# Both column blocks of the HGRN value input made in one opening pass of a float32 decoder block

## The chip, the cores and the metric

One core of one Trainium2 chip runs the whole kernel in one launch. The metric is device time in microseconds (us), lower is better. The kernel before was timed in three runs. One further execution was recorded by the hardware profiler, and all rows shown below come from it.

## The reference

The reference is a decoder block in float32 on 256 tokens of width 1024. Cut to what matters here:

```python
h = rmsnorm(x, attn_norm_g)
proj = h @ w_in                                   # 1024 -> 9216 columns
hq, hf, hi, hg, aq, ak, av, gl = split(proj)      # eight blocks of 1024, the last of 2048
y_hg = hgrn2_mix(hq, hf, hi, hg, lb, out_gain) @ w_branch_hg    # linear recurrence
att  = moba_attention(rmsnorm(aq), rmsnorm(ak), av, rel_table)  # causal, 8 heads of 128
y_at = att @ w_branch_attn
gates = sigmoid(gl)
x = x + (gates[0] * y_hg + gates[1] * y_at) @ w_out
h2 = rmsnorm(x, ffn_norm_g)
x = x + (silu(h2 @ w_gate) * (h2 @ w_up)) @ w_down              # width 2816
```

`hi` is the value input of the recurrence (columns 2048 to 3071 of `w_in`), `hg` its output gate, `av` the attention values, `gl` the two branch gates. The division by the row norm is taken out of the products: they run on `x` times the channel gain, and each result is scaled afterwards by a factor per token, `rx`.

## The kernel before

**Arithmetic.** Each float32 operand is split into a rounded part (`hi`) and the rest (`lo`), and three products (hi hi, hi lo, lo hi) stand for one. For every piece of weight that arrives (`wraw`), ScalarE (ACT) makes the rounded part `whi` by a copy, VectorE (DVE) makes the rest `wlo` by a subtraction, and TensorE (PE) multiplies. `XT` holds the two parts of the input, eight tiles of 128 channels (`kt` 0 to 7).

**Blocks.** `tok_block` (L76) makes 256 tokens by 512 columns with 48 matmuls into two banks of the accumulator. `feat_block` (L86) makes 512 columns by 256 tokens in 32 pairs of matmuls into four banks. `load_w` (L58) fetches a block in two halves of 1 MiB, through three buffers each of `wraw`, `whi` and `wlo`. The accumulator has four banks named `pw` for these blocks, and two each of `ph` and `pa` for smaller work.

**Opening (L119 to L161).** While the input arrives, the first column block of `hi` (columns 2048 to 2559, banks `V0`) is made tile by tile: for each `kt` SyncE (SP) fetches 256 KiB of weight and 128 KiB of `x`. Then `F0`, the first half of the `hf` block, is begun (L209). The rows of `x` (`xtok`, L212) come behind the weights of `F0`; ACT squares and sums them (L216), `rinv` (L180) takes the root, and `rx` follows. `spread` (L185) brings `rx` over to the other axis by two small matmuls on `dg`. `put_tok` (L225) moves `V0` out of its banks into `V`.

**Middle (L498 to L547).** The recurrence is worked off in levels (`hgrn_level`, L315), each a short chain over ACT, PE and DVE, and one `tok_block` stands between two levels so that PE has work. The second column block of `hi` is one of these fillers (L512), then come the two blocks of `Va`, two of the output gate `sg`, and the branch gates `G`. `hgrn_out` (L372) makes the output `o`, sums its squares and takes `ro`; `hgrn_gate` (L394) multiplies `o` by `ro` and `sg` on DVE and transposes it on PE.

**Order.** Every engine works its own queue in a fixed order. The order is fixed when the program is built, by a scheduler that starts from the order of the code. DMAs issued by SP carry one of eight counters in turn, so a DMA waits until the one eight places ahead of it has landed.

Of the kernel before, what the change touches and what calls it, by code (L numbers as in the profile page):

```python
# [7 lines left out]
F32 = mybir.dt.float32  # L8
# [6 lines left out]
P = 128  # L15
# [12 lines left out]
def tile_hgrn2_moba_block(ctx: ExitStack, tc: tile.TileContext, xm, xT, vecs, table, onehot,  # L28
# [22 lines left out]
    def part(pair, k, m):  # L51
        return pair[k // 4][:, k % 4, m, :]
# [23 lines left out]
    def tok_block(w, c0, act, parts=(4, 4), bank=pw):  # L76
        ps = [bank(), bank()]
        for kt, wh, wl in chunks(w, c0, 512, parts):
            for tb in range(2):
                ts = slice(tb * P, (tb + 1) * P)  # L80
                nc.tensor.matmul(ps[tb], part(act, kt, 0)[:, ts], wh, start=(kt == 0), stop=False)  # L81
                nc.tensor.matmul(ps[tb], part(act, kt, 0)[:, ts], wl, start=False, stop=False)  # L82
                nc.tensor.matmul(ps[tb], part(act, kt, 1)[:, ts], wh, start=False, stop=(kt == KT - 1))  # L83
        return ps
# [31 lines left out]
    vec = const.tile([P, 35], F32, name="vec")  # L116
    xTr = big.tile([P, KT, S], F32, name="xTr", tag="T1")
    XT = [big.tile([P, 4, 2, S], F32R, name=f"XT{i}", tag=("XH", "XL")[i]) for i in range(2)]
    raws = [wp.tile([P, 4, 512], F32, name="wraw") for _ in range(2)]  # L119
    nc.scalar.dma_start(vec, vecs)  # L120
    nc.sync.dma_start(raws[0][:, 0, :], w_in[0:P, 2048:2560])
    nc.sync.dma_start(xTr[:, 0:1, :], xT[:, 0:1, :])
    ones = const.tile([P, P], F32, name="ones")
    nc.vector.memset(ones, 1.0)
    root = small.tile([P, 1], F32, name="root")
# [7 lines left out]
    x_parts = [(k, 1) for k in range(6)] + [(6, 2)]
    whs = [wp.tile([P, 4, 512], F32R, name="whi") for _ in range(2)]
    wls = [wp.tile([P, 4, 512], F32R, name="wlo") for _ in range(2)]
    for k0, n in x_parts:
        xs = slice(k0, k0 + n)
        ks = slice(k0 % 4, k0 % 4 + n)
        if k0 > 0:
            nc.sync.dma_start(raws[k0 // 4][:, ks, :],  # L140
                              w_in[k0 * P:(k0 + n) * P, 2048:2560].rearrange("(k p) c -> p k c", p=P))
            nc.sync.dma_start(xTr[:, xs, :], xT[:, xs, :])
    for k0, n in x_parts:
        raw, wh, wl = raws[k0 // 4], whs[k0 // 4], wls[k0 // 4]
        ks = slice(k0 % 4, k0 % 4 + n)
        nc.scalar.copy(wh[:, ks, :], raw[:, ks, :])
        for kt in range(k0, k0 + n):
            x_hi, x_lo = part(XT, kt, 0), part(XT, kt, 1)
            if kt == 0:
                nc.vector.tensor_scalar_mul(x_hi, xTr[:, kt, :], vec[:, kt:kt + 1])  # L150
            else:
                nc.scalar.mul(x_hi, xTr[:, kt, :], vec[:, kt:kt + 1])
            nc.vector.scalar_tensor_tensor(x_lo, xTr[:, kt, :], vec[:, kt:kt + 1], x_hi.bitcast(F32),
                                           op0=OP.mult, op1=OP.subtract)
        nc.vector.tensor_sub(wl[:, ks, :], raw[:, ks, :], wh[:, ks, :].bitcast(F32))
        for kt in range(k0, k0 + n):
            i = kt % 4
            for am, w in ((0, wh), (0, wl), (1, wh)):
                for tb in range(2):
                    nc.tensor.matmul(V0[tb], part(XT, kt, am)[:, tb * P:(tb + 1) * P], w[:, i, :],  # L160
                                     start=(kt == 0 and am == 0 and w is wh), stop=(kt == KT - 1 and am == 1))  # L161

    ones_r = const.tile([P, P], F32R, name="ones_r")
    nc.gpsimd.tensor_copy(ones_r, ones)
# [43 lines left out]

    F0 = feat_block(w_in, 1024, XT, cut=2)  # L209

    xtok = big.tile([P, 2, D], F32, name="xtok", tag="T2")
    nc.sync.dma_start(xtok, xm.rearrange("(b p) c -> p b c", p=P))  # L212
    ss = small.tile([P, 2], F32, name="ss")
    junk = big.tile([P, D], F32, name="junk", tag="T12")
    for tb in range(2):
# [9 lines left out]
    def put_tok(dst, ps, half):  # L225
        for tb in range(2):
            nc.scalar.mul(dst[:, tb, half * 512:(half + 1) * 512], ps[tb], rx[:, tb:tb + 1])

    put_tok(V, V0, 0)


    K = big.tile([P, 2, H, P], F32, name="K", tag="T2")
# [73 lines left out]
    def hgrn_diag_put(qkh, qkl):  # L306
        for tb in range(2):
            for g in range(2):
                bank = ph().rearrange("p (h t) -> p h t", h=4)
                for m, part in enumerate((qkh, qkl)):  # L310
                    nc.tensor.matmul(bank, ones_r, part[:, tb, 4 * g:4 * g + 4, :], start=(m == 0), stop=(m == 1))
                nc.vector.tensor_mul(A[:, tb, 4 * g:4 * g + 4, :], bank,
                                     ident.unsqueeze(1).to_broadcast([P, 4, P]))
# [374 lines left out]
```

## Time and profile before

| | us |
|---|---|
| median of three runs | 505.94 (504.81 to 505.97) |
| the profiled execution, its own time | 506.59 |
| its span in the profile | 504.5 |
| PE busy | 496.2 |
| DVE busy | 332.9 |
| ACT busy | 283.0 |

The span is the time between the first and the last instruction recorded; 2.1 us of the execution's own time lie around it. The profiled execution was 0.65 us slower than the median. PE is the engine of the multiplications; a PE row's duration covers the pipeline, so two matmuls in a row overlap and their cost is read from the distance of their starts.

### The profile page before, as it was taken

The page shows a single profiled execution, that of the slowest core. Times are in us where ns is not written, and L with a number is a line of the kernel's source. Part 1 is how long each engine was busy: PE and PEld are TensorE (multiplying, and loading weights), DVE is VectorE, ACT ScalarE, POOL GpSimd, SP SyncE. Part 2 cuts the span into 40 slices and gives each one's busy share as a digit, 9 for nine tenths or more (in the row PEclk, how much of TensorE's full clock was granted, in tenths as well). Part 3 has the DMA queues.
Part 4 walks back from the last instruction along what each step waited for, and adds up shares of the span by engine and source line. Part 5 has one row for each costly group of instructions (what it writes and reads, how often), then busy time and mean ns, then how long its engine had stood idle before and what let it go on. Part 6 is the DMA issues. An engine that isn't in the chain of part 4 may idle for free.

```text
span 504.5 us, 6639 instructions
## 1 busy us (share of the span) xinstructions
PE 496.2 (98%) x2674; PEld 417.0 (83%) x2674; DVE 332.9 (66%) x380; ACT 283.0 (56%) x418; POOL 20.4 (4%) x41
## 2 busy tenths in 40 slices
PE   8899999999999999999999999999999999999996
PEld 6688888788888888888888887888888888888885
DVE  6569998977698643564447567867645746566372
ACT  5597556787569547954443335675535535544350
POOL 9102200000000000000000000000000000000000
PEclk9999999999999999999999999999999999999999
DMA  7966957525424644185465554566555655653522
GB/s 239 380 219 191 350 177 243 168 83 177 159 75 148 202 161 129 39 307 194 166 211 206 166 168 169 171 199 203 176 172 191 213 176 173 210 161 96 193 88 83
DMA packets 44126, 91.20 MB, mean 181 GB/s; under 512 B 1944, under 2 KB 5048, under 8 KB 44096
## 3 DMA queue, kind: packets, MB, share of 16 engines
q1 hardware_dynamic: 43216, 88.12, 52.6%
q0 software_dynamic: 736, 2.65, 1.7%
q8 instruction: 21, 0.34, 0.3%
q14 instruction: 9, 0.07, 0.0%
q10 hardware_dynamic: 144, 0.02, 0.0%
HBM read 89.70 MB, written 1.07 MB: 180 GB/s over the span
## 4 chain that ended last, share of the span: by engine, by line
PE 93%; DMA 2%; ACT 2%; DVE 1%; SPq 0%; issue 0%; DVEq 0%
PE pw L99 21%; PE pw L81 13%; PE pw L82 13%; PE pw L83 13%; PE pw L98 9%; PE acc L610 4%; PE acc L608 4%; PE acc L609 4%; DMA wraw<-w_in 2%; PE ph L332 2%; PE pw L101 1%; PE ph L382 1%; PE pa L492 1%; PE pa L81 1%; PE pa L82 1%; PE pa L83 1%
## 5 line engine op out<-in xcount | busy, mean ns | idle before, releaser
L56 DVE TENSOR_TENSOR wlo<-wraw,whi 128x2048 fp32r<-128x2048 f32 (+1 forms) x83 | 182.1, 2196 | 111.5 <-ACT whi L55 111.1
L55 ACT CAST whi<-wraw 128x2048 fp32r<-128x2048 f32 (+1 forms) x83 | 151.7, 1829 | 117.9 <-PE pw L83 42.2
L99 PE MATMUL pw<-x2T,whi 128*128 128x512 f32 x352 | 121.9, 398 | 0.0
L98 PE MATMUL pw<-x2T,wlo 128*128 128x256 f32 x308 | 86.5, 281 | 0.0
L81 PE MATMUL pw<-whi,XT 128*128 128x512 f32 x192 | 75.8, 395 | 0.0
L82 PE MATMUL pw<-wlo,XT 128*128 128x512 f32 x192 | 75.2, 392 | 0.0
L83 PE MATMUL pw<-whi,XT 128*128 128x512 f32 x192 | 74.9, 390 | 0.0
L99 PEld LDWEIGHTS pw<-x2T,whi 128*128 128x128 f32 x352 | 63.5, 188 | 12.5
L98 PEld LDWEIGHTS pw<-x2T,wlo 128*128 128x128 f32 x308 | 58.2, 189 | 1.8
L99 PE MATMUL pw<-XT,whi 128*128 128x512 f32 x128 | 44.7, 399 | 0.2 <-DVE Fg L111 0.2
L81 PEld LDWEIGHTS pw<-whi,XT 128*128 128x128 f32 x192 | 36.1, 188 | 7.5
L83 PEld LDWEIGHTS pw<-whi,XT 128*128 128x128 f32 x192 | 36.1, 188 | 7.5
L82 PEld LDWEIGHTS pw<-wlo,XT 128*128 128x128 f32 x192 | 36.1, 188 | 7.3
L608 PE MATMUL acc<-whi,hT 128*128 128x512 f32 x88 | 34.3, 390 | 0.0
L610 PE MATMUL acc<-whi,hT 128*128 128x512 f32 x88 | 34.3, 390 | 0.0
L609 PE MATMUL acc<-wlo,hT 128*128 128x512 f32 x88 | 34.2, 389 | 0.0
L98 PE MATMUL pw<-XT,wlo 128*128 128x256 f32 x112 | 31.5, 281 | 0.0
L99 PEld LDWEIGHTS pw<-XT,whi 128*128 128x128 f32 x128 | 23.3, 188 | 5.1 <-DVE Fg L111 0.5
L98 PEld LDWEIGHTS pw<-XT,wlo 128*128 128x128 f32 x112 | 21.2, 189 | 0.8
L609 PEld LDWEIGHTS acc<-wlo,hT 128*128 128x128 f32 x88 | 16.5, 188 | 3.5
L610 PEld LDWEIGHTS acc<-whi,hT 128*128 128x128 f32 x88 | 16.5, 188 | 3.5
L608 PEld LDWEIGHTS acc<-whi,hT 128*128 128x128 f32 x88 | 16.5, 188 | 3.2
(226 smaller groups left out, 684.2 us busy)
## 6 DMA issues: line engine op xcount, KB each, us to landing
wraw<-w_in SPq DMA_DIRECT2D x32, 1024.0 KB, 5.2
wraw<-w_down SPq DMA_DIRECT2D x11, 1024.0 KB, 4.9
wraw<-w_gate SPq DMA_DIRECT2D x10, 1024.0 KB, 5.2
wraw<-w_up SPq DMA_DIRECT2D x10, 1024.0 KB, 5.1
wraw<-w_at SPq DMA_DIRECT2D x4, 1024.0 KB, 5.0
wraw<-w_hg SPq DMA_DIRECT2D x4, 1024.0 KB, 5.2
wraw<-w_out SPq DMA_DIRECT2D x4, 1024.0 KB, 5.1
wraw<-w_in SPq DMA_DIRECT2D x5, 512.0 KB, 9.2
```

The source lines that it names most:

```text
L55: nc.scalar.copy(hi, src)
L56: nc.vector.tensor_sub(lo, src, hi.bitcast(F32))
L81: nc.tensor.matmul(ps[tb], part(act, kt, 0)[:, ts], wh, start=(kt == 0), stop=False)
L82: nc.tensor.matmul(ps[tb], part(act, kt, 0)[:, ts], wl, start=False, stop=False)
L83: nc.tensor.matmul(ps[tb], part(act, kt, 1)[:, ts], wh, start=False, stop=(kt == KT - 1))
L98: nc.tensor.matmul(ps[ct][:, 0:S], lo[:, i, cs], part(act, kt, 0), start=False, stop=False)
L99: nc.tensor.matmul(ps[ct], hi[:, i, cs], both, start=(kt == 0), stop=(kt == KT - 1))
L101: nc.tensor.matmul(ps[ct][:, 0:S], lo[:, i, cs], part(act, kt, 0), start=False, stop=False)
L332: nc.tensor.matmul(o, KP[:, h, qs], t, start=True, stop=True)
L608: nc.tensor.matmul(acc[tb][half], act[:, j, 0, ts], hi[:, i, cs], start=st, stop=False)
L609: nc.tensor.matmul(acc[tb][half], act[:, j, 0, ts], lo[:, i, cs], start=False, stop=False)
L610: nc.tensor.matmul(acc[tb][half], act[:, j, 1, ts], hi[:, i, cs], start=False, stop=en)
```

## The change

The opening now makes all 1024 columns of `hi`, in four banks (`V0`, `V1`), in one loop over `kt`. Its buffers hold two `kt` of 1024 columns in place of four of 512, which is the same size. From `kt` 2 on, a tile of weight comes as one DMA of 512 KiB. `xtok` is fetched after the weights of `kt` 5 and before those of `kt` 6. `kt` 6 and 7 are multiplied for both halves after both are announced. The second `put_tok` of `V` follows the first. In the middle the filler at L512 is gone, and the blocks behind it move up by one: `Va` takes its place, the output gate takes that of `Va`, the first block of branch gate 1 that of the output gate's second. `Va`, `sg` and `G1` live in other buffers for it. `hgrn_diag_put` alternates between banks `ph` and `pa`.

```diff
+    def first(kind, name):
+        return wp.tile([P, 2, D], kind, name=name)
...
+    xtok = big.tile([P, 2, D], F32, name="xtok", tag="T2")
...
-    nc.sync.dma_start(raws[0][:, 0, :], w_in[0:P, 2048:2560])
+    nc.sync.dma_start(raws[0][:, 0, 0:512], w_in[0:P, 2048:2560])
     nc.sync.dma_start(xTr[:, 0:1, :], xT[:, 0:1, :])
+    nc.sync.dma_start(raws[0][:, 0, 512:D], w_in[0:P, 2560:3072])
...
+    V1 = [pw(), pw()]
+    whs, wls = [], []
+
+    def first_products(ps, half, kt):
+        i, hs = kt % 2, slice(half * 512, (half + 1) * 512)
+        wh, wl = whs[kt // 2], wls[kt // 2]
+        for am, w in ((0, wh), (0, wl), (1, wh)):
+            for tb in range(2):
+                nc.tensor.matmul(ps[tb], part(XT, kt, am)[:, tb * P:(tb + 1) * P], w[:, i, hs],
+                                 start=(kt == 0 and am == 0 and w is wh), stop=(kt == KT - 1 and am == 1))
+
+    for kt in range(KT):
+        i = kt % 2
+        if i == 0:
+            if kt > 0:
+                raws.append(first(F32, "wraw"))
+            whs.append(first(F32R, "whi"))
+            wls.append(first(F32R, "wlo"))
+        raw, wh, wl = raws[-1], whs[-1], wls[-1]
+        ks = slice(kt * P, (kt + 1) * P)
+        if kt > 0:
+            nc.sync.dma_start(xTr[:, kt:kt + 1, :], xT[:, kt:kt + 1, :])
+            for hs in ((slice(0, 512), slice(512, D)) if kt < 2 else (slice(0, D),)):
+                nc.sync.dma_start(raw[:, i, hs], w_in[ks, 2048 + hs.start:2048 + hs.stop])
+        if kt == 5:
+            nc.sync.dma_start(xtok, xm.rearrange("(b p) c -> p b c", p=P))
+        x_hi, x_lo = part(XT, kt, 0), part(XT, kt, 1)
+        if kt == 0:
+            nc.scalar.copy(wh[:, i, 0:512], raw[:, i, 0:512])
+            nc.vector.tensor_scalar_mul(x_hi, xTr[:, kt, :], vec[:, kt:kt + 1])
+        else:
+            nc.scalar.mul(x_hi, xTr[:, kt, :], vec[:, kt:kt + 1])
+            nc.scalar.copy(wh[:, i, 0:512], raw[:, i, 0:512])
+        nc.vector.scalar_tensor_tensor(x_lo, xTr[:, kt, :], vec[:, kt:kt + 1], x_hi.bitcast(F32),
+                                       op0=OP.mult, op1=OP.subtract)
+        nc.scalar.copy(wh[:, i, 512:D], raw[:, i, 512:D])
+        for hs in (slice(0, 512), slice(512, D)):
+            nc.vector.tensor_sub(wl[:, i, hs], raw[:, i, hs], wh[:, i, hs].bitcast(F32))
+        for half in range(2):
+            for k in ((), (6, 7))[kt // 7] if kt > 5 else (kt,):
+                first_products((V0, V1)[half], half, k)
...
-    xtok = big.tile([P, 2, D], F32, name="xtok", tag="T2")
-    nc.sync.dma_start(xtok, xm.rearrange("(b p) c -> p b c", p=P))
...
     put_tok(V, V0, 0)
+    put_tok(V, V1, 1)
...
-                bank = ph().rearrange("p (h t) -> p h t", h=4)
+                bank = (ph, pa)[g]().rearrange("p (h t) -> p h t", h=4)
...
-    put_tok(V, tok_block(w_in, 2048 + 512, XT), 1)
+    Va = big.tile([P, 2, D], F32, name="Va", tag="T1")
+    put_tok(Va, tok_block(w_in, 6144, XT), 0)
     S0, S1 = scores(qtok, qss, kT)
     hgrn_level(3)
-    Va = big.tile([P, 2, D], F32, name="Va", tag="T8")
-    put_tok(Va, tok_block(w_in, 6144, XT), 0)
+    put_tok(Va, tok_block(w_in, 6144 + 512, XT), 1)
     softmax("a", S0, P)
     softmax("b", S1, S)
     hgrn_level(4)
-    put_tok(Va, tok_block(w_in, 6144 + 512, XT), 1)
+    sg = big.tile([P, 2, D], F32, name="sg", tag="T8")
...
+    gate_block(0)
     PT0, PT1 = probs_T(S0, S1)
     hgrn_level(5)
-    sg = big.tile([P, 2, D], F32, name="sg", tag="T1")
-
-    def gate_block(half):
-        ps = tok_block(w_in, 3072 + half * 512, XT)
-        for tb in range(2):
-            nc.scalar.activation(sg[:, tb, half * 512:(half + 1) * 512], ps[tb], AF.Silu, scale=rx[:, tb:tb + 1])
-
-    gate_block(0)
+    gate_block(1)
     aT = values(Va, PT0, PT1)
     hgrn_level(6)
-    gate_block(1)
+
+
+    G[1] = big.tile([P, 2, D], F32, name="G1", tag="T11")
+    branch_gate(1, 0)
     A01 = hgrn_cross()
     o, ro = hgrn_out(A01)
-
-
-    G = [None, None]
-    for br in (1, 0):
-        G[br] = big.tile([P, 2, D], F32, name=f"G{br}", tag=("T5", "T6")[br])
-        for half in range(2):
-            ps = tok_block(w_in, 7168 + br * D + half * 512, XT)
-            for tb in range(2):
-                nc.scalar.activation(G[br][:, tb, half * 512:(half + 1) * 512], ps[tb], AF.Sigmoid,
-                                     scale=rx[:, tb:tb + 1])
-            if br == 1 and half == 0:
-                oT = hgrn_gate(o, ro, sg)
+    branch_gate(1, 1)
+    oT = hgrn_gate(o, ro, sg)
+    G[0] = big.tile([P, 2, D], F32, name="G0", tag="T6")
+    branch_gate(0, 0)
+    branch_gate(0, 1)
```

**PE, at the end of `hi`.** `pw` are the banks of `hi` (`XT_75` holds `kt` 4 to 7), then of `F0` (`XT_74` holds `kt` 0 to 3), and `ph<-dg` is the matmul of `spread`. Before:

```order
L160 MATMUL pw<-whi,XT_75 128x512 x4
L160 MATMUL pw<-wlo,XT_75 128x512 x2
L160 MATMUL pw<-whi,XT_75 128x512 x2
L99 MATMUL pw<-XT_74,whi 128x512
L101 MATMUL pw<-XT_74,wlo 128x256
L98 MATMUL pw<-XT_74,wlo 128x256
```

Now:

```order
L149 MATMUL pw<-whi,XT_75 128x512 x3
L149 MATMUL pw<-wlo,XT_75 128x512 x2
L149 MATMUL pw<-whi,XT_75 128x512 x2
L210 MATMUL ph<-dg,ones 128x128
L149 MATMUL pw<-whi,XT_75 128x512 x3
L149 MATMUL pw<-wlo,XT_75 128x512 x2
L149 MATMUL pw<-whi,XT_75 128x512 x3
L149 MATMUL pw<-wlo,XT_75 128x512 x2
L149 MATMUL pw<-whi,XT_75 128x512 x2
L210 MATMUL ph<-dg,ones 128x128
L99 MATMUL pw<-XT_74,whi 128x512
```

The first matmul of `spread` stands between the products of `kt` 6 and those of `kt` 7; before, both stood behind all of `F0`.

**ACT, around the squares of `xtok`.** Before:

```order
L152 ACTIVATE XT_75<-xTr,vec 128x256 x2
L55 CAST whi<-wraw 128x1024 x4
L110 COPY Fg<-pw 128x2x128
L216 ACTIVATE junk,ss<-xtok 128x1024
L182 ACT_TABLE_LOAD
L182 ACTIVATE rx<-rx 128x2
L55 CAST whi<-wraw 128x2048
L227 ACTIVATE V<-pw,rx 128x512 x2
```

Now:

```order
L234 ACTIVATE junk,ss<-xtok 128x1024
L172 ACTIVATE XT_75<-xTr,vec 128x256
L234 ACTIVATE junk,ss<-xtok 128x1024
L173 CAST whi<-wraw 128x512
L176 CAST whi<-wraw 128x512
L172 ACTIVATE XT_75<-xTr,vec 128x256
L202 ACT_TABLE_LOAD
L202 ACTIVATE rx<-rx 128x2
L173 CAST whi<-wraw 128x512
L176 CAST whi<-wraw 128x512
L55 CAST whi<-wraw 128x1024 x2
L245 ACTIVATE V<-pw,rx 128x512
```

The squares now stand ahead of the copies of `kt` 6, and the root for `rx` ahead of the copies of `kt` 7, which PE needs for `hi`.

**DVE, at the output of the recurrence.** `ro` is the factor of the output norm. Before:

```order
L56 TENSOR_TENSOR wlo<-wraw,whi 128x2048 x2
L181 TENSOR_SCALAR ro<-so 128x16
L183 RECIPROCAL ro<-ro 128x16
L398 SCALAR_TENSOR_TENSOR o<-o,ro,sg 128x128 x16
L56 TENSOR_TENSOR wlo<-wraw,whi 128x2048
```

Now:

```order
L56 TENSOR_TENSOR wlo<-wraw,whi 128x2048 x2
L201 TENSOR_SCALAR ro<-so 128x16
L56 TENSOR_TENSOR wlo<-wraw,whi 128x2048
L203 RECIPROCAL ro<-ro 128x16
L417 SCALAR_TENSOR_TENSOR o<-o,ro,sg 128x128 x16
```

A split of a weight half has moved in between the two steps of `ro`. On PE the sixteen transposes of `o` (L406) stood in one piece; now seven matmuls of the running block stand among them.

## Rows read from the trace of the kernel before

**Rows 1.** The page: busy time of each engine, then the chain that ended last.

```profile
PE 496.2 (98%) x2674; PEld 417.0 (83%) x2674; DVE 332.9 (66%) x380; ACT 283.0 (56%) x418; POOL 20.4 (4%) x41
...
PE 93%; DMA 2%; ACT 2%; DVE 1%; SPq 0%; issue 0%; DVEq 0%
```

**Rows 2.** Stretches: length, busy of each engine, granted clock, DMA share, GB/s.

```profile
0.00:8.00 8.00, 5.81 (x23) 4.74 (x24) 3.76 (x13) 3.71 (x7) 7.03 (x19) 1.00 0.71 209
8.00:16.00 8.00, 6.78 (x30) 5.26 (x28) 5.16 (x12) 5.20 (x11) 5.89 (x16) 1.00 0.93 308
9.00:14.00 5.00, 5.00 (x24) 4.14 (x23) 3.81 (x8) 2.77 (x6) 4.89 (x13) 1.00 0.85 259
16.00:24.00 8.00, 7.84 (x39) 6.33 (x40) 6.54 (x7) 4.60 (x5) 0.00 (x0) 1.00 1.05 400
```

**Rows 3.** Timeline of PE in the opening: start, duration, line, operation, idle before.

```profile
4.91 0.70 PE L160 MATMUL pw<-whi,XT 128*128 128x512 f32 x2
...
7.69 0.73 PE L160 MATMUL pw<-whi,XT 128*128 128x512 f32 x2 [1.04 <-ACT XT L152]
...
9.63 0.62 PE L160 MATMUL pw<-wlo,XT 128*128 128x512 f32 x2
...
10.99 0.62 PE L160 MATMUL pw<-wlo,XT 128*128 128x512 f32 x2
...
19.29 0.39 PE L99 MATMUL pw<-XT,whi 128*128 128x512 f32 x1
```

**Rows 4.** Timeline of PE in the two `hf` blocks, up to the first of Q.

```profile
31.04 0.60 PE L190 MATMUL ph<-dg,ones 128*128 128x128 f32 x4
31.40 0.82 PE L99 MATMUL pw<-XT,whi 128*128 128x512 f32 x2
...
32.89 0.39 PE L101 MATMUL pw<-XT,wlo 128*128 128x256 f32 x1
...
41.00 0.28 PE L98 MATMUL pw<-XT,wlo 128*128 128x256 f32 x1
...
41.35 0.28 PE L98 MATMUL pw<-XT,wlo 128*128 128x256 f32 x1
...
43.59 0.63 PE L99 MATMUL pw<-XT,whi 128*128 128x512 f32 x2
```

**Rows 5.** Timeline of ACT, then of DVE, in the opening.

```profile
10.86 0.62 ACT L146 CAST whi<-wraw 128x512 fp32r<-128x512 f32 x1
11.38 0.51 ACT L152 ACTIVATE XT<-xTr,vec 128x256 fp32r<-128x256 f32 x1
...
26.04 1.07 ACT L216 ACTIVATE junk<-xtok 128x1024 f32<-128x1024 f32 x1
...
27.21 1.28 ACT L182 ACT_TABLE_LOAD   x1
28.51 0.20 ACT L182 ACTIVATE rx<-rx 128x2 f32<-128x2 f32 x1
...
29.02 0.48 DVE L189 TENSOR_SCALAR dg<-ident,rx 128x128 f32<-128x128 f32 x2
```

**Rows 6.** SP's issue of `xtok`; then DMA issues up to 40 us: size, us to landing.

```profile
12.48 0.86 SPq L212 DMA_DIRECT2D xtok<-xm  x1
...
xtok<-xm SPq DMA_DIRECT2D x1, 1024.0 KB, 11.0
```

**Rows 7.** Timeline of ACT, DVE and PE at the output of the recurrence.

```profile
206.53 1.28 ACT L182 ACT_TABLE_LOAD   x1
...
207.95 1.90 ACT L55 CAST whi<-wraw 128x2048 fp32r<-128x2048 f32 x1
...
208.43 4.29 DVE L398 SCALAR_TENSOR_TENSOR o<-o,ro,sg 128x128 f32<-128x128 f32 x16
212.64 2.28 DVE L56 TENSOR_TENSOR wlo<-wraw,whi 128x2048 fp32r<-128x2048 f32 x1
...
211.84 0.60 PE L406 MATMUL pa<-ident,o 128*128 128x128 f32 x4
```

More of the change, by code (lines that the diff above doesn't have):

```diff
@@ L118, in tile_hgrn2_moba_block @@
     XT = [big.tile([P, 4, 2, S], F32R, name=f"XT{i}", tag=("XH", "XL")[i]) for i in range(2)]
-    raws = [wp.tile([P, 4, 512], F32, name="wraw") for _ in range(2)]
+    def first(kind, name):
+        return wp.tile([P, 2, D], kind, name=name)
+    xtok = big.tile([P, 2, D], F32, name="xtok", tag="T2")
+    raws = [first(F32, "wraw")]
     nc.scalar.dma_start(vec, vecs)
-    nc.sync.dma_start(raws[0][:, 0, :], w_in[0:P, 2048:2560])
+    nc.sync.dma_start(raws[0][:, 0, 0:512], w_in[0:P, 2048:2560])
     nc.sync.dma_start(xTr[:, 0:1, :], xT[:, 0:1, :])
+    nc.sync.dma_start(raws[0][:, 0, 512:D], w_in[0:P, 2560:3072])
     ones = const.tile([P, P], F32, name="ones")
@@ L132, in tile_hgrn2_moba_block @@
     V0 = [pw(), pw()]
[L133 to L158, printed above, removed]
-                for tb in range(2):
-                    nc.tensor.matmul(V0[tb], part(XT, kt, am)[:, tb * P:(tb + 1) * P], w[:, i, :],
-                                     start=(kt == 0 and am == 0 and w is wh), stop=(kt == KT - 1 and am == 1))
+    V1 = [pw(), pw()]
@@ L519, in tile_hgrn2_moba_block @@
     hgrn_level(4)
-    put_tok(Va, tok_block(w_in, 6144 + 512, XT), 1)
-    PT0, PT1 = probs_T(S0, S1)
-    hgrn_level(5)
-    sg = big.tile([P, 2, D], F32, name="sg", tag="T1")
+    sg = big.tile([P, 2, D], F32, name="sg", tag="T8")
     def gate_block(half):
@@ L528, in gate_block, with branch_gate @@
             nc.scalar.activation(sg[:, tb, half * 512:(half + 1) * 512], ps[tb], AF.Silu, scale=rx[:, tb:tb + 1])
+    G = [None, None]
+    def branch_gate(br, half):
+        ps = tok_block(w_in, 7168 + br * D + half * 512, XT)
+        for tb in range(2):
+            nc.scalar.activation(G[br][:, tb, half * 512:(half + 1) * 512], ps[tb], AF.Sigmoid,
+                                 scale=rx[:, tb:tb + 1])
     gate_block(0)
+    PT0, PT1 = probs_T(S0, S1)
+    hgrn_level(5)
+    gate_block(1)
     aT = values(Va, PT0, PT1)
     hgrn_level(6)
-    gate_block(1)
+    G[1] = big.tile([P, 2, D], F32, name="G1", tag="T11")
+    branch_gate(1, 0)
     A01 = hgrn_cross()
     o, ro = hgrn_out(A01)
-    G = [None, None]
-    for br in (1, 0):
-        G[br] = big.tile([P, 2, D], F32, name=f"G{br}", tag=("T5", "T6")[br])
-        for half in range(2):
-            ps = tok_block(w_in, 7168 + br * D + half * 512, XT)
-            for tb in range(2):
-                nc.scalar.activation(G[br][:, tb, half * 512:(half + 1) * 512], ps[tb], AF.Sigmoid,
-                                     scale=rx[:, tb:tb + 1])
-            if br == 1 and half == 0:
-                oT = hgrn_gate(o, ro, sg)
+    branch_gate(1, 1)
[3 more added lines that the diff above has]
+    branch_gate(0, 1)
     M = [big.tile([P, 4, 2, S], F32R, name=f"M{i}", tag=("T8", "T9")[i]) for i in range(2)]
```

## The prediction

> **What bounds the kernel now.** I read the page first: PE is busy 496.2 of 504.5 us, and 93% of the chain that ended last are PE rows [rows 1]. So time can be won only where PE does not multiply, and time is lost wherever PE is made to wait; DVE and ACT have room on average. Next I read the table of stretches. The granted clock is 1.00 throughout, the upper of its two levels, so nothing is to be had there. PE is short of work at the start: 5.81 of the first 8 us, part of which is warming up on constants, and 6.78 of the second 8 [rows 2]. The timeline of PE shows why. Useful work begins at 4.91, then PE idles for inputs, the first time 1.04 us, and reaches `F0` only at 19.29 [rows 3]. The DMA share over these stretches is 0.93 to 1.05 while the rate goes from 209 over 308 to 400 GB/s [rows 2]: the opening waits for its data.
>
> I use one marker for everything: the first matmul of the Q block, the second of the two that start at 43.59, so 43.82 [rows 4]. A matmul of a token block costs 0.227 us: six lie between the starts 9.63 and 10.99 [rows 3]. A pair of a feature block costs 0.35, the distance from 41.00 to 41.35 [rows 4]. From 4.91 to 43.82 are 38.91 us. The work in them is 48 x 0.227 = 10.9 for `V0`, 64 pairs x 0.3515 = 22.5 for the two `hf` blocks, and 0.36 for the four matmul passes of `spread` (31.04 to 31.40) [rows 4]. The other 5.2 us are lost or go to the small table product L260: 3.5 before `F0` (19.29 - 4.91 - 10.9), 1.0 around L260 (two matmuls from 31.40 end at 31.86, the next row starts at 32.89), and 0.7 elsewhere in the two `hf` blocks.
>
> **The change, part by part.** *The moved block.* The second half of `hi` is 48 matmuls wherever it stands, 48 x 0.227 = 10.9 us. Before, with that block counted in, PE had done as much as now at the marker by 43.82 + 10.9 = 54.7. What the change can win is the difference between 54.7 and the new start of the Q block, if the middle then runs as it did.
>
> *The opening's data.* A `kt` now brings 655 KB (128 KiB of `x`, 512 KiB of weight) and 12 matmuls, 2.72 us, in place of 393 KB and 1.36 us. PE then needs 241 GB/s in place of 289. ACT has for each `kt` three instructions of 0.62, 0.62 and 0.51 [rows 5], DVE about as much; both fit under 2.72. In the first two `kt` PE still waits for pieces of 256 KiB: the second weight piece stands where the weight of `kt` 1 stood, and PE resumed on that at 7.69 [rows 3]; I put the end of `kt` 1 at 11.7 (4.91 + 24 x 0.227 = 10.4, and 1.3 waited). From there PE has data in hand: the weights of `kt` 3 end at 2.62 MB in the queue, and 1.67 MB have moved by 8 us [rows 2], so at 259 GB/s, the slowest stretch, they are through at 11.7 and landed by 13.8, when PE is at 14.4. So PE would reach `kt` 6 at 11.7 + 4 x 2.72 = 22.6.
>
> *The rows of `x`.* `xtok` now stands in the middle of the opening, and the chain from it to `rx` ends in a matmul that stands on PE's queue ahead of `kt` 7. Everything behind it on PE (the last 12 matmuls, then `F0`) waits for that chain. `xtok` ends at 4.98 MB in the queue. By the rates of before, 4.13 MB by 16 us and then 400 GB/s [rows 2], its last byte is through at 18.1. Before, it ended at 6.29 MB, so 21.4, and landed 11.0 us behind its issue at 12.48, at 23.5 [rows 6]; the lag is 2.1, and I put the new landing at 20.2. If the larger pieces ran at 400 GB/s from 8 us on, it would be 18.4.
> On ACT two squares and one scaled copy follow: 1.07 + 0.4 + 1.17 (26.04 to 27.21) [rows 5], 2.65 us, to S = 22.85 (or 21.05). Then come the two copies of `kt` 6 (1.1), a scaled copy (0.4), the table load 1.28, the root 0.2, and 0.8 to the first `dg` on DVE (28.51 to 29.02, and its own length) [rows 5], so S + 3.7. PE spends the first part of it on `kt` 6, whose copies come first. After that `kt` 7 takes 2.72, its copies lag by 0.2, and the `spread` matmuls cost 0.2 each, so `F0` starts at about S + 6.8. The four `pw` banks are full of `hi`; `F0` needs the first one emptied by ACT, which also ends near S + 6.8. With S = 22.85 that is 29.65. With the early landing PE itself is the limit: 22.6 + 24 x 0.227 + 0.4 = 28.4. I take 29.0, the middle, because the slow stretch of before (9 to 14 us) has no cause that I could name [rows 2].
>
> Against such a chain speaks the Trainium skill, ScalarE: Activation LUTs, section "What ACT_TABLE_LOAD costs": it puts a drain of about 1.38 us on top of the load. The trace disagrees: the root starts at 28.51, 0.02 behind a load of 1.28 that began at 27.21 [rows 5]. By the Trainium skill's figure `F0` would be 1.4 us later and the gain as much smaller; the measurement decides, and the figure gets no chance below.
>
> *Behind it.* `F0` and `F1` are 22.5. L260 keeps its place at the Q block and a bank wait or two may remain: 0.6 to 1.3, I take 0.9, near the 1.0 of before. The Q block starts at 29.0 + 22.5 + 0.9 = 52.4. The gain at the marker is 54.7 - 52.4 = 2.3, from 54.7 - 53.45 = 1.2 to 54.7 - 51.5 = 3.2.
>
> *The middle.* Between any two levels there is still exactly one filler block of the same size, with the same loads on SP and the same splits; the fillers only change names. The new buffers (T1, T8, T11) were last read well before. The sigmoid table is loaded once more on ACT, 1.28 us, while ACT waits for PE's block: nothing, as long as ACT waits there. One place costs something. At the output of the recurrence the squares end at 206.53 and the sixteen products on DVE began at 208.43 [rows 7]. Now a copy (1.90) stands ahead of the table load and its split (2.28) [rows 7] ahead of the second step of `ro`, so the products begin at 206.5 + 1.9 + 2.3 + 0.4 = 211.1 and end 4.29 later at 215.4. PE comes to the transposes at 211.84; with seven matmuls among them (1.6) and 1.75 for themselves it would be through at 215.2. So PE loses about 0.2; I bound it by 0 and 0.5. The alternating banks of the diagonal only remove waits; before, PE did not stand still there, so nothing.
>
> *Sum.* 2.3 - 0.2 = 2.1 us less, between 0.75 and 3.2. The profiled execution took 506.59, so 504.5 for one like it; it was 0.65 above the median, and the sum does not depend on that, so against the median of 505.94 I say **503.8**.
>
> **The rivals.** *A, the data comes too late (slower).* If the larger opening keeps the rate of the stretch from 9 to 14 us, 259 GB/s [rows 2], `xtok` lands at 8 + 3.31/0.259 + 2.1 = 22.9, S is 25.5, `F0` starts at 32.3 and the Q block at 55.7, so 1.0 us later than before, 1.2 with the gate: 507.1. It decides below about 285 GB/s from 8 us on. For it speaks that rate, over five microseconds with the share at 0.85; against it, 400 GB/s right behind it with DMAs of 512 KiB. The Trainium skill, DMA: Bandwidth & Descriptors, section "Bandwidth", asks for 1 MiB in one DMA for 75% of the peak and would set the opening's smaller pieces below that; by the trace 512 KiB pieces run at 400.
> *B, the gain is spent in the middle.* If at the gate DVE's split waits for its copy a further 1.3 us (the table load ahead of it) or some level loses its cover, the gain falls to some 0.9: 505.0. For it speaks how tight the place is (0.2 us); against it, that before no filler left PE idle there.
> *C, the change does not do what it says.* The opening is fed, but the banks of `hi` are emptied late, since casts of `F0` stand between the four copies on ACT; each cast of 1024 columns costs about 1.0, one or two of them on the path: gain 0.6 to 1.1, 505.1.
> *D, no wait at all.* `F0` at 4.91 + 96 x 0.227 + 0.4 = 27.1, gain 54.7 - 27.1 - 23.1 = 4.5, less 0.2: 501.6. It would need the first two `kt` without waits, which the landing of the first pieces speaks against.
>
> **How the numbers follow.** A measurement of this kernel can tell a change of about 0.3%, 1.5 us, from none. I give my forecast 0.56, A 0.12, B 0.16, C 0.10, D 0.06. Of the forecast's own range (0.75 to 3.2 gained, so 502.7 to 505.2) 0.04 lies within 1.5 us. Faster: 0.52 + 0.06 + 0.02 of B = 0.60. Slower: 0.07, the worse part of A. Within: the rest, 0.33. For the range I leave out the worse half of A and most of D, and allow half a microsecond for the median's own scatter: 502.2 to 506.3.
>
> **What would show it.** In the changed kernel's trace the first matmul of `F0` should start near 29, that of Q near 52.4, and the row of the first `spread` matmul should show at most 1 us of idle PE ahead of it, waiting on DVE. The first square of `xtok` should start between 18.4 and 20.2; a start behind 22 means A. The idle time of PE ahead of `kt` 1 (1.04) should be split into smaller ones, and there should be none from there to `kt` 6. Idle PE between copies of `V` on ACT at the start of `F0` means C; idle PE at the transposes of `o` above half a microsecond means B. I am wrong if the Q block starts on time and the end does not move with it.

## The result

The changed kernel takes 502.58 us (median of six runs, 502.43 to 503.35), the kernel before 505.87 in the same comparison (504.81 to 506.01). The ratio is 0.994, with a 95% interval of 0.9923 to 0.9957: faster by some 3 us, where the prediction had 2.1. The profiled execution took 503.10 us with a span of 501.3, against 506.59 and 504.5.

The page of the changed kernel, the lines that answer to [rows 1]:

```profile
PE 495.4 (99%) x2674; PEld 416.5 (83%) x2674; DVE 334.3 (67%) x387; ACT 285.2 (57%) x426; POOL 21.8 (4%) x41
...
PE 95%; ACT 3%; DMA 1%; SPq 0%; issue 0%; DVE 0%; DVEq 0%
```

PE does the same 2674 instructions in a span that is 3.2 us shorter, and its share goes from 98 to 99%. The stretches of the changed kernel, with the columns of [rows 2]:

```profile
0.00:8.00 8.00, 6.75 (x27) 5.29 (x28) 4.28 (x15) 3.45 (x6) 7.03 (x19) 1.00 0.68 201
8.00:16.00 8.00, 7.80 (x34) 5.80 (x33) 6.79 (x13) 6.99 (x14) 6.56 (x16) 1.00 1.04 402
9.00:14.00 5.00, 5.00 (x22) 3.78 (x22) 4.43 (x9) 4.18 (x9) 5.00 (x11) 1.00 1.04 401
16.00:24.00 8.00, 8.00 (x37) 6.64 (x36) 4.06 (x11) 6.54 (x13) 0.00 (x0) 1.00 1.04 390
```

PE is busy for 7.80 us of the second eight, where it was 6.78, and the stretch from 9 to 14 us runs at 401 GB/s in place of 259. The timeline of PE, changed kernel, answers to [rows 3] and [rows 4]:

```profile
4.92 0.70 PE L149 MATMUL pw<-whi,XT 128*128 128x512 f32 x2
...
8.75 0.73 PE L149 MATMUL pw<-whi,XT 128*128 128x512 f32 x2 [0.20 <-ACT whi L173]
...
25.51 0.39 PE L210 MATMUL ph<-dg,ones 128*128 128x128 f32 x2
...
28.48 0.39 PE L210 MATMUL ph<-dg,ones 128*128 128x128 f32 x2
28.62 0.48 PE L99 MATMUL pw<-XT,whi 128*128 128x512 f32 x1
...
51.33 0.59 PE L279 MATMUL pa<-oh,tb_sb 32*8 32x256 f32 x2
51.85 0.50 PE L99 MATMUL pw<-XT,whi 128*128 128x512 f32 x1
```

`F0` starts at 28.62, Q at 51.85, and neither matmul of `spread` has idle time ahead of it. ACT in the same stretch, answering to [rows 5]:

```profile
17.90 1.06 ACT L234 ACTIVATE junk<-xtok 128x1024 f32<-128x1024 f32 x1 [1.43 <-DMA xtok<-xm]
...
19.36 1.04 ACT L234 ACTIVATE junk<-xtok 128x1024 f32<-128x1024 f32 x1
...
21.95 1.28 ACT L202 ACT_TABLE_LOAD   x1
23.25 0.20 ACT L202 ACTIVATE rx<-rx 128x2 f32<-128x2 f32 x1
...
27.31 0.69 ACT L245 ACTIVATE V<-pw,rx 128x512 f32<-128x512 f32 x1 [0.93 <-PE pw L149]
```

`xtok` is there at 17.9. The copies of `V` wait for PE (0.93 us), not PE for them. With four marks on PE the 3.2 us can be followed through the program. For the first three, where the moved block has not yet run in the kernel before, its 10.9 us are added there. The fourth column is the experiment `move_alone`, told below.

| first matmul of | before | changed | `move_alone` | lead of changed |
|---|---|---|---|---|
| Q | 43.82 + 10.9 = 54.72 | 51.85 | 54.04 | 2.9 |
| transposes of the scores S | 160.39 + 10.9 = 171.29 | 168.36 | 170.57 | 2.9 |
| transposes of `o` | 211.84 + 10.9 = 222.74 | 218.91 | 221.11 | 3.8 |
| transposes of the gated sum `G` | 269.64 | 266.46 | 268.66 | 3.2 |
| end of the span | 504.5 | 501.3 | 503.5 | 3.2 |

So 2.9 us are won up to Q, 0.9 between the scores and the output of the recurrence, and 0.6 are lost again at the gate. Of the 2.9, 1.6 stand at `F0` (19.29 + 10.9 against 28.62), and 1.3 come between `F0` and Q (24.53 us before, 23.23 now). How much is won up to Q depends on the execution of the old opening: against that of `move_alone` it is 2.2.

### The profile page after: what moved, and what is told of

Its sections match the earlier page's. It is cut to its first block, busy times and chain, and to the rows that moved or that the text cites. A ratio compares the mean times of both kernels' runs of the same rounds, so it can differ in the third digit from the quotient of the medians.

```text
span 501.3 us, 6658 instructions
## 1 busy us (share of the span) xinstructions
PE 495.4 (99%) x2674; PEld 416.5 (83%) x2674; DVE 334.3 (67%) x387; ACT 285.2 (57%) x426; POOL 21.8 (4%) x41
## 4 chain that ended last, share of the span: by engine, by line
PE 95%; ACT 3%; DMA 1%; SPq 0%; issue 0%; DVE 0%; DVEq 0%
PE pw L99 22%; PE pw L81 12%; PE pw L82 12%; PE pw L83 12%; PE pw L98 10%; PE acc L633 4%; PE acc L631 4%; PE acc L632 4%; PE pw L149 4%; PE ph L351 2%; PE pw L101 1%; DMA wraw<-w_in 1%; PE pa L83 1%; PE pa L82 1%; PE pa L81 1%; PE pa L511 1%
## 5 line engine op out<-in xcount | busy, mean ns | idle before, releaser
L56 DVE TENSOR_TENSOR wlo<-wraw,whi 128x2048 fp32r<-128x2048 f32 (+1 forms) x81 | 176.6, 2185 | 115.8 <-ACT whi L55 115.5
L55 ACT CAST whi<-wraw 128x2048 fp32r<-128x2048 f32 (+1 forms) x81 | 147.8, 1827 | 113.9 <-PE pw L83 39.3
L81 PE MATMUL pw<-whi,XT 128*128 128x512 f32 x176 | 69.9, 397 | 0.0
L82 PE MATMUL pw<-wlo,XT 128*128 128x512 f32 x176 | 69.2, 393 | 0.0
L83 PE MATMUL pw<-whi,XT 128*128 128x512 f32 x176 | 69.0, 392 | 0.0
L81 PEld LDWEIGHTS pw<-whi,XT 128*128 128x128 f32 x176 | 33.1, 188 | 6.8
L82 PEld LDWEIGHTS pw<-wlo,XT 128*128 128x128 f32 x176 | 33.1, 188 | 6.5
L83 PEld LDWEIGHTS pw<-whi,XT 128*128 128x128 f32 x176 | 33.1, 188 | 6.6
```

The lines of the kernel that those rows point to most:

```text
L55: nc.scalar.copy(hi, src)
L56: nc.vector.tensor_sub(lo, src, hi.bitcast(F32))
```

## The experiments

### Is it the opening, or the move?

`move_alone` takes the change apart: the old opening, the moved block as an ordinary one ahead of Q, and the new middle. Against the changed kernel, cut to its core:

```diff
-    V1 = [pw(), pw()]
...
+    x_parts = [(k, 1) for k in range(6)] + [(6, 2)]
...
-    put_tok(V, V1, 1)
...
+    put_tok(V, tok_block(w_in, 2048 + 512, XT), 1)
     Q = big.tile([P, 2, H, P], F32, name="Q", tag="T1")
```

> One part alone: the opening of the kernel before (`V0` only, its DMAs, `xtok` behind `F0`'s weights), with the second block of `hi` as an ordinary block between `F1` and Q, and the middle as in the changed kernel (`Va`, `sg` and `G1` moved up by one block, alternating banks of the diagonal). Theory (all that Q gains comes from the one pass of the opening; moving a block elsewhere frees nothing, and the new middle differs by +0.9 us won around levels 5 and 6 and 0.6 lost at the gate): Q at 54.3 to 55.2, S transposes to transposes of `o` 50.5 us (51.45 before), end 0.2 to 0.6 us before that of the kernel before, time 505.0 to 505.6. Rival (half or more of the gain comes from the move, as covers fit better): time at or below 504.2.

Measured: 505.51 us (504.97 to 506.65), 1.0013 of the kernel before (1.0001 to 1.0025). Q starts at 54.04. From the scores' transposes to those of `o` it takes 50.54 us, as in the changed kernel (50.55; before 51.45), and from there to `G` 47.55, as in the changed kernel (47.55; before 57.80 - 10.9 = 46.9). **The move brings no gain that a time shows; the new opening brings it.** Which part of the opening does is the next question. The two smaller differences, 0.9 won and 0.6 lost, belong to the new order of the middle. Q stood 0.7 us ahead of the kernel before and 0.3 ahead of the expected range, since this execution of the old opening was quicker: `F0` started at 17.63.

### Is it the form of the DMAs?

Two kernels exchange the forms. `small_pieces` gives the changed opening small weight DMAs again:

```diff
-            for hs in ((slice(0, 512), slice(512, D)) if kt < 2 else (slice(0, D),)):
+            for hs in ((slice(0, 512), slice(512, D)) if kt < 8 else (slice(0, D),)):
```

`before_pairs` gives the old opening large ones:

```diff
-    x_parts = [(k, 1) for k in range(6)] + [(6, 2)]
+    x_parts = [(0, 1), (1, 1), (2, 2), (4, 2), (6, 2)]
```

> Edit: in the changed kernel the weights of every `kt` of the opening come as two DMAs of 256 KiB, as before the change, instead of one of 512 KiB from `kt` 2 on. Rival (the form of the DMAs made the opening fast): the stretch from 9 to 14 us falls from 401 GB/s back to 260 to 310, `xtok` lands near 20 instead of 17.9, and Q starts 0.5 to 1.5 us later than at 51.85; time 503.1 to 504.0. Theory (the second column block gives PE 12 matmuls per 655 KB, so that 241 GB/s are enough): whatever the rate does, PE goes without idle time from `kt` 2 on and Q starts within 0.4 us of 51.85; time 502.6.

> Edit: the kernel before, with the weights and `x` of `kt` 2 and 3, and of 4 and 5, fetched and split in pairs as those of 6 and 7 are (512 and 256 KiB in a DMA instead of 256 and 128). It asks whether larger DMAs alone would have given the gain, with no block moved. If the stretch from 9 to 14 us was slow because of the small pieces: it goes from 259 to about 400 GB/s, the last tile lands near 14, `F0` starts near 17.5 instead of 19.29 and Q near 42.0 instead of 43.82; time 504.1. If the gain comes from PE having twice the work for each tile (my theory): `F0` starts at 18.8 to 19.8, Q within 0.5 us of 43.82, time within 0.6 us of the kernel before.

Stretches of `small_pieces`, with the columns of [rows 2]; the last two divide the time from 7 to 14 us:

```profile
8.00:16.00 8.00, 8.00 (x37) 6.53 (x36) 7.44 (x14) 6.94 (x14) 7.23 (x16) 1.00 1.01 353
9.00:14.00 5.00, 5.00 (x23) 4.14 (x23) 4.91 (x9) 4.28 (x9) 5.00 (x10) 1.00 1.00 334
...
7.00:12.00 5.00, 4.98 (x22) 3.69 (x22) 4.97 (x11) 4.50 (x9) 5.00 (x11) 1.00 1.05 384
12.00:14.00 2.00, 2.00 (x10) 1.68 (x9) 1.91 (x4) 1.43 (x4) 2.00 (x5) 1.00 0.91 254
```

One of `before_pairs`:

```profile
9.00:14.00 5.00, 3.35 (x15) 2.72 (x16) 3.62 (x5) 3.40 (x7) 4.87 (x13) 1.00 1.05 398
```

And its timeline of PE, the longest wait and the start of `F0`:

```profile
10.65 0.72 PE L160 MATMUL pw<-whi,XT 128*128 128x512 f32 x2 [1.66 <-ACT XT L152]
...
18.98 0.39 PE L99 MATMUL pw<-XT,whi 128*128 128x512 f32 x1
```

`small_pieces`: from 9 to 14 us the rate fell to 334 GB/s, PE went on without idle time, and Q started at 51.22, 0.2 us earlier than the theory allowed. Its time was 503.22 us (502.87 to 503.60), ratio 0.9961 (0.9948 to 0.9974). That lies in the range of the rival, some half a microsecond above the changed kernel (502.58 and 502.76). In the profiled execution this half microsecond came behind the last matmul, where the end of the span stood 4.6 us away instead of 4.1, and not in the opening; the other executions have no profile, so it stays open what the small pieces cost in time.

`before_pairs`: the rate rose to 398 GB/s, the time stayed at 505.63 (505.39 to 505.91), ratio 1.0005 (0.9992 to 1.0018). PE had to wait 1.66 us for the first pair, was 0.3 us earlier at `F0` and 0.5 earlier at Q. So large DMAs alone gain nothing, and without them 2.4 of the 3 us remain (503.22 against 505.60 for the kernel before in the same comparison): **the gain follows from the work that PE has for each tile.**

The low rate goes with the old form of the DMAs (259 GB/s before, 314 in `move_alone`, 334 here; 375 to 404 in the runs with the new DMAs), but it is not the rate of small pieces as such. In `small_pieces` they run at 384 GB/s from 7 to 12 us, and at 254 from 12 to 14: the average hides a slow spell. In the three executions with the old form such a spell falls between 10 and 14 us; in the nine with larger pieces none does, though `gate_again` has one from 8 to 10 (252 GB/s). Its cause is open. Small pieces also mean fewer bytes under way, since a DMA of SP waits for the one eight places ahead (in the kernel before the eleventh was issued at 6.61, when the third had landed at 6.59), and no run separates that from their size. The old opening is exposed to such a spell: `F0` started at 19.29 in one execution and at 17.63 in `move_alone`, with the same DMAs up to there, though only 0.7 of these 1.7 us were left at Q. That would also fit the wider scatter of the kernel before, 504.2 to 507.3 in the last comparison, but no run tests it.

### Is the place of `xtok` worth anything?

`x_late` fetches the rows of `x` behind the weights of `kt` 7, that is behind the loop:

```diff
-        if kt == 5:
-            nc.sync.dma_start(xtok, xm.rearrange("(b p) c -> p b c", p=P))
...
+    nc.sync.dma_start(xtok, xm.rearrange("(b p) c -> p b c", p=P))
     ones_r = const.tile([P, P], F32R, name="ones_r")
```

`x_early` fetches them ahead of the weights of `kt` 4:

```diff
-        if kt == 5:
+        if kt == 3:
```

> Edit: in the changed kernel `xtok` is fetched behind the weights of `kt` 7 instead of ahead of those of `kt` 6, so 1.31 MB stand ahead of it more. At the 0.40 MB/us of the changed kernel's stretch from 8 to 24 us it lands 3.3 us later, at about 21.2. The order then puts both `spread` matmuls directly ahead of `F0`. Theory (PE alone sets the start of `F0`; the chain over `rx` had some 1.3 us of slack and the position of `xtok` matters little): squares end near 23.7, `dg` near 26.2, PE comes to it near 28.2, so `F0` starts at 28.6 and Q at 51.9, both within 0.4 of the changed kernel, and the time is the same, 502.6. Rival (the prediction's chain, S + 6.8, sets `F0`): `F0` at 30.5, Q at 53.7, time 504.5.

> Edit: in the changed kernel `xtok` is fetched ahead of the weights of `kt` 4 instead of those of `kt` 6 (1.31 MB earlier, 1.05 MB more ahead of `kt` 4 and 5). Theory (the place in the queue is a balance: the 1 MiB delays the tiles behind it by 2.6 us, and PE's data in hand ahead of `kt` 4 is less than that): `kt` 4 lands near 16.9, ACT is through with the squares near 17.3, so PE comes to `kt` 4 near 18 instead of 15.7 and idles 1.5 to 2.5 us; `F0` at 29.8 to 30.8, time 504.0 to 505.0. Rival (the opening has data to spare at 400 GB/s): no idle PE, `F0` within 0.4 of 28.4, time 502.6.

The timeline of PE in `x_late`, at the start of `F0`:

```profile
27.77 0.61 PE L210 MATMUL ph<-dg,ones 128*128 128x128 f32 x4
30.01 0.50 PE L99 MATMUL pw<-XT,whi 128*128 128x512 f32 x1 [1.63 <-ACT V L245]
```

And of its ACT, from the second square to the copies of `V`:

```profile
22.25 1.06 ACT L234 ACTIVATE junk<-xtok 128x1024 f32<-128x1024 f32 x1
...
25.04 1.28 ACT L202 ACT_TABLE_LOAD   x1
26.34 0.20 ACT L202 ACTIVATE rx<-rx 128x2 f32<-128x2 f32 x1
26.45 2.92 ACT L55 CAST whi<-wraw 128x1024 fp32r<-128x1024 f32 x3
29.28 2.41 ACT L245 ACTIVATE V<-pw,rx 128x512 f32<-128x512 f32 x4
```

Measured: 504.08 us (503.68 to 504.65), ratio 0.9971 (0.9961 to 0.9982), `F0` at 30.01, Q at 53.27. My theory for this run fell. The squares ended at 23.4, and `F0` came 6.6 behind them, close to the 6.8 of the prediction's rule, but that agreement is chance: the rule counts the copies and products of `kt` 6 and 7 behind the squares, and here they stood ahead of them. I had counted only the chain to `dg`, which was in time: `spread` ran at 27.77 without a wait. But `F0` needs a bank that ACT has emptied, the factor for that is the root at 26.34, and three casts of `F0`'s weights (2.92 us) stand ahead of the copies. That is the mechanism of rival C, in a kernel where `rx` comes late.

`x_early`: 503.74 us (503.64 to 504.29), ratio 0.9968 (0.9954 to 0.9982). Its timeline of PE at `kt` 4:

```profile
17.53 1.02 PE L149 MATMUL pw<-whi,XT 128*128 128x512 f32 x3 [0.48 <-ACT whi L173]
```

PE waits ahead of `kt` 4, as expected, but for less than the 1.5 to 2.5 us: its matmuls would have gone on at 16.88 (the last two of `kt` 3 start at 16.43, 0.227 each) and went on at 17.53, so 0.65 are lost, most of the 0.9 by which `F0`, at 29.11 (29.8 to 30.8 expected), trails the changed kernel run beside it (28.20, below). ACT was through with its cast at 17.47, as worked out; PE came there later than the 15.7 that I had counted. The time is 0.3 us below the expected range. Both directions cost, 1.0 us early and 1.3 late against 502.76 for the changed kernel (below; `x_late` ran in another comparison): **the place of `xtok` is part of the gain.**

### What was lost at the gate?

The changed kernel at the gate, answering to [rows 7]; first the timeline of DVE:

```profile
217.99 0.24 DVE L203 RECIPROCAL ro<-ro 128x16 f32<-128x16 f32 x1
218.27 4.29 DVE L417 SCALAR_TENSOR_TENSOR o<-o,ro,sg 128x128 f32<-128x128 f32 x16
```

Then that of PE:

```profile
218.91 0.27 PE L425 MATMUL pa<-ident,o 128*128 128x128 f32 x1
...
219.81 0.48 PE L82 MATMUL pw<-wlo,XT 128*128 128x512 f32 x1
220.13 0.40 PE L83 MATMUL pw<-whi,XT 128*128 128x512 f32 x1
...
222.50 0.49 PE L425 MATMUL ph<-ident,o 128*128 128x128 f32 x3
222.75 0.49 PE L82 MATMUL pw<-wlo,XT 128*128 128x512 f32 x1
223.07 0.39 PE L83 MATMUL pw<-whi,XT 128*128 128x512 f32 x1
```

In the kernel before, the second matmul behind the transposes of `o`:

```profile
213.82 0.40 PE L82 MATMUL pw<-wlo,XT 128*128 128x512 f32 x1
```

Sixteen transposes and eight matmuls take 223.07 - 218.91 = 4.16 us. Before, sixteen and one took 1.98 (211.84 to 213.82), so 1.98 + 7 x 0.227 = 3.57 would do, and 0.59 are lost. No row shows idle time, since the rows overlap. Two readings offer themselves: the alternation costs (0.32 from a matmul behind a transpose to the next, in place of 0.227), or PE waits for the products. `gate_one_piece` writes the transposes behind the first block of `G0`, cut to its core:

```diff
+    def hgrn_gate_T(o):
...
-    oT = hgrn_gate(o, ro, sg)
+    hgrn_gate(o, ro, sg)
     G[0] = big.tile([P, 2, D], F32, name="G0", tag="T6")
     branch_gate(0, 0)
+    oT = hgrn_gate_T(o)
     branch_gate(0, 1)
```

`gate_in_pieces` spreads them over the second block, two behind every three matmuls, long after the products are done. `hook` is called behind each third product in `tok_block`, and `pieces` makes two transposes at each call. Against `gate_one_piece`, cut to its core:

```diff
-    oT = hgrn_gate_T(o)
-    branch_gate(0, 1)
+    oT = []
+    pieces = hgrn_gate_T(o, oT)
+    branch_gate(0, 1, hook=lambda: next(pieces, None))
```

> Edit: in the changed kernel the products of `hgrn_gate` stay where they are, but its sixteen transposes and their copies are written behind the first block of `G0`, so that they stand in one piece on PE again, as before the change. In the changed kernel PE lost 0.6 us of its lead at the transposes of `o`, where they alternate with seven matmuls. Theory (the alternation, or waiting for the products, costs this 0.6 us): it is regained, PE's lead behind the gate goes from 3.2 to 3.8 us, time 502.0. Rival (the loss has moved to the block behind, because the splits of `oT` come later and something waits for them): time 502.6 or more.

> Edit: as in the run with the transposes of `o` in one piece, but they stand in eight pieces of two, each behind three matmuls of the second block of `G0`, some 12 us after the products of `o` are done, so nothing waits for data. A matmul of 512 columns behind a transpose starts 0.32 us before the next matmul, otherwise 0.227. Theory (the alternation itself costs: 0.09 us for every return from a small matmul to a large one): eight returns in place of one, 0.65 us longer for this stretch than in one piece. Rival (the 0.64 us at the gate were waiting for the products on DVE): no difference from one piece, within 0.1 us.

The timeline of PE in `gate_in_pieces`, one round:

```profile
230.28 0.38 PE L428 MATMUL pa<-ident,o 128*128 128x128 f32 x2
230.41 0.48 PE L81 MATMUL pw<-whi,XT 128*128 128x512 f32 x1
230.73 0.39 PE L82 MATMUL pw<-wlo,XT 128*128 128x512 f32 x1
230.96 0.39 PE L83 MATMUL pw<-whi,XT 128*128 128x512 f32 x1
231.19 0.38 PE L428 MATMUL pa<-ident,o 128*128 128x128 f32 x2
```

A round of two transposes and three matmuls takes 0.91 us, and 2 x 0.109 + 3 x 0.227 is 0.90. What the matmul behind a transpose seems to lose, the transposes ahead of it had gained. From the scores' transposes to those of `G` it takes 98.10 us in the changed kernel, 97.44 in one piece and 97.59 in eight. **Alternation costs at most 0.15 us for seven returns, not the 0.65 of my theory; the 0.6 at the gate were waiting for the products.** The rows agree: of the three transposes from 222.50 on, 0.109 apart, the last starts at 222.72, right behind the last product (218.27 + 4.29 = 222.56). The times are 502.27 (502.05 to 502.59; ratio 0.9943, 0.9928 to 0.9959) and 502.28 (502.07 to 502.42; ratio 0.9934, 0.9919 to 0.9948).

The version in one piece was run once more.

> The changed kernel with the transposes of `o` in one piece behind the first block of `G0`, once more with more rounds, as the version that would beat both kernels. By the markers of its first run it stands 0.6 us ahead of the changed kernel (502.58 and 502.76 in two comparisons): expected 502.1, ratio to before 0.993. If the 0.6 us were a matter of one profiled execution: 502.6.

Measured: 502.08 us (501.71 to 502.20), ratio 0.9937 (0.9925 to 0.9950), and the stretch from the scores to `G` again 97.45. It is 0.6 us ahead of the changed kernel by the marks. The times say the same, but their intervals overlap.

### The alternating banks, and the changed kernel once more

`diagonal_on_ph` undoes one line:

```diff
-                bank = (ph, pa)[g]().rearrange("p (h t) -> p h t", h=4)
+                bank = ph().rearrange("p (h t) -> p h t", h=4)
```

> Edit: in the changed kernel `hgrn_diag_put` uses the banks of `ph` alone again, as before the change. The order then has its eight matmuls in three pieces with matmuls of the running block between them, where the changed kernel has them in one. The prediction put nothing on the alternating banks. Theory (each return to the block costs 0.09 us, and a bank has to be emptied before it is written again): 0.2 to 0.4 us longer from Q to the transposes of `ktok`, which are 58.47 apart in the changed kernel. Rival (the prediction): 0.0. The time cannot tell these apart; the marker in the trace can.

Measured: 502.95 us (502.83 to 503.05), ratio 0.9947 (0.9933 to 0.9961). From Q to the transposes of `ktok` it takes 58.61 us, against 58.47: 0.14, between the two expectations. In seven other runs with the alternating banks it is 58.46 to 58.48 (in `x_early`, where another order stands ahead of Q, 58.39), so the banks are worth something, but little.

The changed kernel without an edit:

> The changed kernel once more, unedited, beside the other runs of this group: how far its opening varies from one profiled execution to the next, and its time for comparison. In the recorded executions so far with the same first two tiles, `F0` started at 28.62, 28.33 and 28.00. Expected: `F0` between 28.0 and 28.7, Q between 51.2 and 51.9, 15.8 to 16.2 us from the transposes of `o` onward unchanged, time 502.3 to 502.9.

Measured: 502.76 us (502.37 to 503.04), ratio 0.9943 (0.9929 to 0.9958); `F0` at 28.20, Q at 51.43, 98.05 us from the scores to `G`. (The figure of 15.8 to 16.2 us in the expectation was a slip; nothing rests on it.) Over the six executions with this opening, this one, the first, the three of the gate and `diagonal_on_ph`, Q started between 51.12 and 51.85.

## Why the prediction was right, point by point

**The bound and the mechanism** held. PE is the bound, the old opening starved it, and 12 matmuls for each 655 KB feed it. The rows list one wait up to `F0`, 0.20 us at `kt` 1; by the starts 1.6 us are lost there in all (28.62 - 4.92 less 96 x 0.227 and 0.3 for `spread`), nearly all in the first two `kt`, where I had put 1.3. Before the change it was 3.5. `move_alone` shows that the moved block and the new middle carry no gain by themselves.

**The data.** I took the middle between the slow stretch and 400 GB/s, for lack of a cause. With the new DMAs the stretch ran at 401; the slow spell of before did not come, and its cause is still open. (The Trainium skill, DMA: Bandwidth & Descriptors, section "Bandwidth", wants 1 MiB in one DMA for 75% of the peak. The traces show no such need for DMAs issued in a row: pieces of 512 KiB made 401 GB/s, and pieces of 128 and 256 KiB 384, outside the slow spell.) `xtok` was there at 17.9 (18.4 in my early case), the squares ended at 20.4 (21.05), and PE alone set the start of `F0`. For that case I had 28.4, and 27.89 to 28.62 were read. The value taken, 29.0, was 0.4 to 1.1 too late.

**The chain over `rx`** has 1.4 us of slack by my rule (20.4 + 6.8 = 27.2 against 28.62), so it did not decide, and no run tests the rule: in `x_late` its number came out to 0.2 by chance, while the emptied bank set `F0`. (Nor does the changed kernel show the drain of 1.38 us that the Trainium skill, ScalarE: Activation LUTs, section "What ACT_TABLE_LOAD costs", puts on top of a load: the load ends at 21.95 + 1.28 = 23.23, and the root starts at 23.25.)

**Behind `F0`** I had 23.4 and 23.23 were read, though the table product (L260, now L279) did not keep its place, as I had it: before it stood at the head of `F1` and cost 1.0, now it stands directly ahead of Q, and Q starts 0.52 behind it. The gain at Q was 2.9 instead of 2.3, within 1.2 to 3.2; against the quicker old opening of `move_alone` it was 2.2.

**The middle** was mis-sized twice, in opposite directions. At the gate I had 0.2, bounded by 0.5, and 0.6 was lost. The start of the products was right (0.64 us ahead of PE's arrival; worked out 0.74), and so was the amount of PE work under them, 3.34 us against products that end 3.65 behind PE's arrival. By these numbers 0.3 were to be lost (3.65 - 3.34). What failed is the step that let PE go on as soon as the last product ends: behind that end (222.56) came the last transpose and a matmul, and the next one in full step started only at 223.07, which is the other 0.3 (0.51 less the matmul's own 0.227). And "nothing" for the other levels missed 0.9 us between the scores and `o`: 0.36 up to the first product with `Va` (175.62 before, 183.23 now), 0.32 from there to L368 (193.54; now L387, 200.83), 0.22 behind it. Each of the three stretches holds 48 matmuls of the running blocks in both kernels, so the difference lies in the smaller ones. In the kernel before, the timeline of PE is broken up there:

```profile
160.39 1.03 PE L481 MATMUL pa<-ident,S 128*128 128x128 f32 x8
161.36 0.56 PE L332 MATMUL ph<-QA,KP 128*64 128x64 f32 x10
161.85 1.10 PE L481 MATMUL pa<-ident,S 128*128 128x128 f32 x8
162.88 0.91 PE L332 MATMUL ph<-QA,KP 128*64 128x64 f32 x22
163.72 0.50 PE L81 MATMUL pw<-whi,XT 128*128 128x512 f32 x1
```

In the changed kernel's timeline of PE, level 5 is one piece:

```profile
168.36 1.03 PE L500 MATMUL pa<-ident,S 128*128 128x128 f32 x8
169.32 1.15 PE L351 MATMUL ph<-QA,KP 128*64 128x64 f32 x32
170.40 0.50 PE L81 MATMUL pw<-whi,XT 128*128 128x512 f32 x1
...
171.21 1.03 PE L500 MATMUL pa<-ident,S 128*128 128x128 f32 x8
172.00 0.48 PE L81 MATMUL pw<-whi,XT 128*128 128x512 f32 x1
```

The 32 small matmuls take 0.49 + 0.84 = 1.33 us in two pieces and 1.08 in one, and the second group of transposes 1.03 against 0.79. Level 6 repeats it: the same 32 came in two pieces (18 and 14, 1.33 us) and come in one now (1.08). The traces speak against waits for banks here. Changing from transposes to the small matmuls takes the same time in both kernels: eight transposes last 0.97 and 0.96 us when small matmuls follow, 0.79 when a matmul of the block does. And in the trace of the kernel before, neither the first matmul of the second piece nor its weight load waits for a semaphore, at either level. The old order changes over twice at each level, the new one once. `move_alone` shows that the 0.9 comes with the new order; what the 0.22 at the output consist of stays open.

**The sum.** I had 2.3 - 0.2 = 2.1; read were 2.9 + 0.9 - 0.6 = 3.2. The forecast's own range ended at 502.7, and 502.58 lies just below it; the half microsecond allowed for scatter holds it. So the mechanism of the opening was right, and the time came out as near as it did because an error of 0.4 at the gate made up for part of the 0.9 that I had put at nothing.

**The rivals.** A (data too late) fell with the rate of 401. B has its place right and its mechanism wrong: the products were not late by a further 1.3 us, and no other level lost its cover, yet the gate lost 0.6, above the half microsecond that was to be its sign. C did not occur here, but does as soon as `rx` is 3 us later. D did not occur; the waits of the first two tiles are still there.

## What to carry over

Where the engine that bounds a kernel starves at the start, give it more work for each tile that arrives; larger DMAs alone raised the rate and did not help, since the waits only moved. Then look at what must arrive for the next stage, and put it into the queue where it neither delays the tiles nor releases the banks late: here 1.3 MB earlier or later each cost a microsecond. And compare the distance of marks between two kernels, not only the idle times that a view lists, for half a microsecond, a wait or a change between two kinds of matmul, can lie hidden between rows that overlap.

## What the runs showed of the hardware

DMAs of 128 and 256 KiB issued in a row ran at 384 GB/s from 7 to 12 us in `small_pieces` and at 254 from 12 to 14; with the weights in 512 KiB pieces the stretch from 9 to 14 ran at 375 to 404 in nine executions, with the same issuing engine. Transposes of 128 columns and matmuls of 512 can alternate on PE at no cost that the marks show above 0.15 us for eight pieces, though the start of the second matmul behind a transpose comes 0.09 us late. Small matmuls with 64 columns of weights are another matter: the same 32, between matmuls of 128, took 1.33 us in two pieces and 1.08 in one, though the second piece waited for no semaphore. From the last matmul to the end of the span it took 3.9 to 4.2 us in eleven of the twelve recorded executions, and 4.6 in one.
